# Attention, out-projection and FFN of one encoder layer: the last gate norm in block 0's FFN, two output tiles' SSD halves ahead, and two gate products by token halves

## The chip, the cores and the metric

One core of one Trainium2 chip runs the whole program. The metric is the device time of one execution in microseconds; the time of a kernel is the median of its runs. A core has a matrix engine (PE), a vector engine (DVE), an activation engine (ACT), a general engine (POOL) and a queue engine (SP), which in this kernel only issues the DMAs. Each engine executes its own program in order and waits on semaphores of the others.

## The reference

One encoder layer over 2048 new frames and 32 running streams of one frame-step each. What matters here (`p` are the weights, names shortened):

```python
def mixer(h, k_past, v_past, ssm_h0, conv_prev, p):
    proj = h @ p['w_in']                  # q, k, v, z, x/B/C, dt
    ...
    attn = stick_breaking(q, q_pos, k_all, v_all, k_pos).reshape(b, l, D_ATT)
    ...
    y, h_fin = ssd_scan(xh, dt, a, bm, cm, ssm_h0)
    y = y + p['d_skip'][:, None] * xh
    y = rmsnorm(y * jax.nn.silu(z), p['g_ssm_out'])
    out = jnp.concatenate([rmsnorm(attn, p['g_attn_out']), y], axis=-1) @ p['w_out']
    ...
def conv_ffn(h, conv_prev, p):
    gu = h @ p['w_up']
    gate_c, conv_new = causal_dwconv(gu[..., :D_FF], conv_prev, p['ffn_conv_w'], p['ffn_conv_b'])
    return (jax.nn.gelu(gate_c, approximate=True) * gu[..., D_FF:]) @ p['w_down'], conv_new
...
x = x + rmsnorm(mixer(rmsnorm(x)))        # pre and post norm, each with its gain
x = x + rmsnorm(conv_ffn(rmsnorm(x)))
```

`D_MODEL` is 1024, `D_FF` 2816; 8 attention heads and 8 SSD heads of 64. The out-projection multiplies a row of 1024 values: 512 of attention and 512 of SSD.

## The kernel before

Tokens are cut into four blocks of 512, 512, 512 and 544 (the last holds the 32 running streams). Features lie on partitions, 128 at a time, tokens in the free dimension. Every large product is done in three matmuls of fp32r parts, high by high, high by low and low by high (`dense`, L173 to L186, the matmul is L180), so a product over 1024 inputs (8 pieces `k` of 128) is 24 matmuls for one tile of 128 outputs. Weights are split into parts once (`divide`: cast on ACT L160, subtraction on POOL L161, store L164) and read back from DRAM later (`recall`, L152).

`phase_in` (0 to 595 us) makes the input projections and the SSD of all blocks. What is left of it is the gate of block 3: `gate` multiplies by the weights of z, 32 steps of 6 matmuls of 128x272, and applies the gate; `gate_norm` (L680 to L706) squares, sums over partitions (L222), takes the power on POOL (L245), transposes back (L257), scales on DVE (L698), makes high and low parts on ACT and POOL (L702, L704) and stores both to `yS[3]` (L705, L706).

`heads(s)` is the attention of block s: slots of one head, one block of keys and 128 queries. A slot is scores (L914), a log-sigmoid pair on ACT (L759, L760), a scan (L762) and a product (L767) on DVE or POOL, transposes on PE (L933) that ACT casts and DVE subtracts from (L937, L938), and the products with v (L955), added to `att` on DVE (L970). Block 0 has 32 slots, block 1 64. Between slots `heads` takes steps of a filler, a generator that writes other work into the program; the number of steps per slot is a fixed rate: L1576 to L1594 give `heads(0)` the gate and the norm, 44 steps, and `heads(1)` the stream of block 0, 648. PE's products of a filler are pinned behind the attention's matmuls that precede them; each engine's order then comes from a scheduler that simulates the program.

`Tail.stream(0)`, the filler of `heads(1)`: `out_units` makes the 8 output tiles c of the out-projection for token half a, then for half b, each over k = 4..7 (SSD) and then 0..3 (attention, which needs all heads of block 0 and their norm). Half a's chain runs beside half b's products: `residual` (sums L222, transposes L257, scaling L1072 on DVE, addition L1077, store L1078), `split` (high part xhi on ACT L1107, low part xlo on DVE L1108) and `root` (second sums and power). Half b's chain then runs beside GAP = 24 empty steps (L1485 to L1489), and only then do the FFN's products begin, by `up(j)`: 22 pairs of gate product (PSUM tile `o`, two banks) and up product (tile `u`), then `down`. The gate product's result goes to `gb` on DVE (L1335) with r, the root of the norm, as a factor, so that it waits for both halves' `root`.

Lines that the diff touches stand in the profile under the numbers printed here.

## Time and profile before

| | us |
|---|---|
| median of three runs | 2865.14 |
| lowest, highest | 2861.31, 2866.26 |
| the profiled execution | 2866.48 |
| its span in the trace | 2864.7 |
| block 0's attention (from the first slot) | 595.02 to 686.99 |
| start of block 1's attention to the dense out-projection | 686.99 to 717.75 |
| sums of half a | 743.35 |
| end of half b's out products | 767.9 |
| first gate result (L1335), first up product | 805.23, 805.5 |

Over the span PE is busy for 97%, DVE 58%, ACT 43%, POOL 40%. A row of the timeline is one instruction or several equal ones in a row; the brackets at its end say how long the engine had been idle and what ended that. In tables by stage, "busy" counts an instruction from start to end at whatever clock PE had, and PEclk is the mean share of the full clock.

### The profile page before, as it was taken

To read this page: it belongs to the slowest core of one execution; us is meant where nothing else is said; L and a number is where in the kernel's file an instruction comes from. 1 tells how busy PE (TensorE), PEld (TensorE's weight loads), DVE (VectorE), ACT (ScalarE), POOL (GpSimd) and SP (SyncE) were. 2 spreads that over 40 slices of the span, in tenths; PEclk is the share of its full clock that TensorE was granted. 3 is DMA by queue.
4 is the path that set the end of the run, shared out by engine and by line. 5 is a ranking of instruction groups with operands and counts; after the bars stand their busy time and mean duration, and the time that the engine had idled before them with its cause. 6 is when DMAs were issued, how large, how long until landed. Compare 5 with 4: busy or idle time off the path is not lost.

```text
span 2864.7 us, 45898 instructions
## 1 busy us (share of the span) xinstructions
PE 2772.8 (97%) x16673; PEld 2393.9 (84%) x16673; DVE 1648.3 (58%) x2628; ACT 1218.0 (43%) x2570; POOL 1142.8 (40%) x1075
## 2 busy tenths in 40 slices
PE   7999999998899999999999999999999999999998
PEld 6777879986878888897888888878888878899998
DVE  7684747368564455657555555876666653623334
ACT  5343434357655454555433334644444433321211
POOL 4633241325666565655322224553323224511113
PEclk9999999999999999999999999999999999999999
DMA  8879595997868877876655557665555555755554
GB/s 297 283 257 312 201 314 179 289 283 242 299 197 290 272 255 259 282 257 200 202 181 181 180 177 246 201 207 186 175 174 168 167 188 189 252 177 177 173 181 129
DMA packets 342083, 635.73 MB, mean 222 GB/s; under 512 B 73082, under 2 KB 188418, under 8 KB 332386
## 3 DMA queue, kind: packets, MB, share of 16 engines
q1 hardware_dynamic: 341282, 632.24, 67.8%
q8 instruction: 133, 2.18, 0.3%
q14 instruction: 92, 0.75, 0.1%
q10 hardware_dynamic: 576, 0.56, 0.1%
HBM read 476.11 MB, written 156.57 MB: 221 GB/s over the span
## 4 chain that ended last, share of the span: by engine, by line
PE 81%; DMA 7%; DVE 6%; issue 2%; ACT 2%; POOL 1%; SPq 1%; DVEq 0%; POOLq 0%; ACTq 0%
PE o L180 41%; PE u L180 13%; PE t L180 11%; PE z L914 4%; PE pa L955 4%; PE pt L933 3%; PE o L451 3%; DMA w<-wS_outw 1%; DVE prow L762 1%; DMA w<-wS_wq 1%; DMA acB<-acD 1%; DMA eA<-acD 1%; DMA w<-wS_outw_part 1%; DVE xlo L1108 1%; PE u L222 1%
## 5 line engine op out<-in xcount | busy, mean ns | idle before, releaser
L180 PE MATMUL o<-xhi,w 128*128 128x512 f32 (+2 forms) x3968 | 1038.9, 344 | 20.4 <-ACT xhi L353 7.9
L180 PEld LDWEIGHTS o<-xhi,w 128*128 128x128 f32 x3968 | 694.6, 191 | 112.4 <-ACT xhi L353 7.9
L180 PE MATMUL o<-xlo,w 128*128 128x512 f32 (+2 forms) x1984 | 681.0, 344 | 3.4 <-DVE xlo L354 1.2
L767 POOL TENSOR_TENSOR beta<-beta,prow 128x512 f32<-128x512 f32 (+3 forms) x256 | 256.1, 1001 | 505.2 <-DVE prow L762 443.2
L180 PEld LDWEIGHTS o<-xlo,w 128*128 128x128 f32 x1984 | 377.4, 190 | 48.2 <-DVE xlo L339 3.0
L180 PE MATMUL u<-xhi,w 128*128 128x512 f32 x1056 | 351.4, 398 | 0.0
L180 PE MATMUL o<-ah,w 128*128 128x512 f32 x992 | 341.7, 402 | 7.0 <-DVE f L1410 7.0
L1356 POOL TENSOR_TENSOR y<-y,gb 128x512 f32<-128x512 f32 (+1 forms) x88 | 115.8, 1315 | 445.6 <-ACT gb L1355 442.8
L161 POOL TENSOR_TENSOR w<-wraw,w 128x512 fp32r<-128x512 f32 (+3 forms) x180 | 244.5, 1361 | 122.4 <-ACT w L160 92.2
L938 DVE TENSOR_TENSOR wt<-pt,wt 128x512 fp32r<-128x512 f32 (+2 forms) x320 | 192.2, 602 | 150.2 <-ACT wt L937 148.7
L762 DVE TENSOR_TENSOR_SCAN prow<-gam,prow,z 128x513 f32<-128x513 f32 x192 | 245.3, 1278 | 55.5 <-ACT beta L760 55.2
L937 ACT CAST wt<-pt 128x512 fp32r<-128x512 f32 (+2 forms) x320 | 168.0, 526 | 234.3 <-PE pt L933 232.1
L180 PEld LDWEIGHTS u<-xhi,w 128*128 128x128 f32 x1056 | 198.6, 188 | 46.1
L180 PEld LDWEIGHTS o<-ah,w 128*128 128x128 f32 x992 | 187.1, 189 | 49.2 <-DVE f L1410 7.9
L180 PE MATMUL u<-xlo,w 128*128 128x512 f32 x528 | 209.1, 396 | 0.0
L180 PE MATMUL o<-al,w 128*128 128x512 f32 x496 | 196.9, 397 | 0.0
L759 ACT ACTIVATE gam<-z 128x512 f32<-128x512 f32 (+2 forms) x320 | 173.3, 542 | 52.3 <-PE z L914 28.5
L180 PE MATMUL t<-xhi,w 128*128 128x272 f32 x960 | 189.5, 293 | 6.1 <-DMA w<-wS_outw_part 3.4
L933 PE MATMUL pt<-ident,beta 128*128 128x128 f32 x1088 | 182.8, 277 | 1.8 <-DVE wt L938 1.0
L1348 DVE SCALAR_TENSOR_TENSOR y<-gb,cv,y 128x512 f32<-128x512 f32 (+1 forms) x176 | 143.9, 818 | 66.0 <-ACT y L1346 63.0
L160 ACT CAST w<-wraw 128x512 fp32r<-128x512 f32 (+3 forms) x180 | 113.5, 631 | 160.8 <-PE o L180 94.3
L955 PE MATMUL pa<-wt,v 128*64 128x256 f32 (+3 forms) x1152 | 171.4, 279 | 9.9 <-DVE wt L938 4.3
(290 smaller groups left out, 4846.6 us busy)
## 6 DMA issues: line engine op xcount, KB each, us to landing
w<-wS_up SPq DMA_DIRECT2D x264, 512.0 KB, 3.6
w<-wS_dn SPq DMA_DIRECT2D x144, 384.0 KB, 3.5
wS_up<-w SPq DMA_DIRECT2D x88, 512.0 KB, 3.3
w<-wS_outw SPq DMA_DIRECT2D x78, 512.0 KB, 6.3
wraw<-wup SPq DMA_DIRECT2D x88, 256.0 KB, 4.4
k<-kS SPq DMA_DIRECT2D x80, 256.0 KB, 3.8
v<-vS SPq DMA_DIRECT2D x80, 256.0 KB, 3.8
w<-wS_bx SPq DMA_DIRECT2D x18, 1024.0 KB, 4.9
```

The lines of the kernel that those rows point to most:

```text
L161: nc.gpsimd.tensor_tensor(lo, raw[:, :m, :], hi.bitcast(F32), op=ALU.subtract)
L180: mm = nc.tensor.matmul(ps[:, : c1 - c0], l, r, start=first and i == 0 and k == 0, stop=last and i == 2 and k == len(w) - 1, **({"skip_gro ...
L759: nc.scalar.activation(g[:, c0:512], z, AF.Sigmoid, scale=-0.125)
L762: nc.vector.tensor_tensor_scan(back(pr), back(g), z[:, 0:1].to_broadcast([P, n + 1]), self.kn.ones[:, 0:1] if prev is None else prev, op0= ...
L767: eng.tensor_tensor(b[:, :n], b[:, :n], pr[:, c0 + 1 : 513], op=ALU.mult)
L914: mm = nc.tensor.matmul(z[:, :n], q[:, P * b : P * b + P], k[:, :n], start=e == 0, stop=e == 1 and kc < s)
L933: mm = nc.tensor.transpose(t[:, P * j : P * j + P], w[:, P * j : P * j + P], kn.ident[:])
L937: nc.scalar.copy(hi, t)
L938: kn.exit = nc.vector.tensor_tensor(lo, t, hi.bitcast(F32), op=ALU.subtract)
L955: nc.tensor.matmul(av[:m, 2 * P * p + c0 : 2 * P * p + 2 * P], v[:, j, :m], wt[:, rest, j, c0:], start=kc == s and p + j + rest == 0, stop ...
L1348: nc.vector.scalar_tensor_tensor(y[:, :W], gb[:, i : i + W], kn.col(wc + i), y[:, :W], op0=ALU.mult, op1=ALU.add)
L1356: nc.gpsimd.tensor_tensor(y[:, :W], y[:, :W], t, op=ALU.mult)
```

## The change

Three things move.

1. The norm of block 3's gate. `gate` still fills block 0's attention (36 steps instead of 44), but each of its four tiles is stored to DRAM (`yG`); `gate_norm_last` loads them back as `gx` in two tiles of 272 tokens, and its steps (28 for both) are taken as `done` steps in block 0's FFN.
2. In `stream(0)`, after ten empty steps, `out_ahead` opens both `o` banks with output tiles 0 and 1: their SSD halves (k = 4..7) on all 512 tokens, then their attention halves by token halves. `out_units` makes the other six.
3. `gates` takes the place of the empty steps but eight: the gate products of j = 0 and 1 on the first 256 tokens, while half b's chain runs. `up(0)` and `up(1)` complete them on the last 256.

```diff
+        if s == NSB - 1:
+            nc.sync.dma_start(kn.yG[:, c, :], xc[:, c, :nt])
...
+def gate_norm_last(kn, tmp, pool):
+
+    nc, s = kn.nc, NSB - 1
+    for c0, c1 in tiles_of(SBS[s][1]):
+        n = c1 - c0
+        tile = lambda nm, bufs=1: pool.tile([P, n], F32, name=nm, bufs=bufs)
+        xs, sq = [], tile("gsq")
+        for c in range(4):
+            xs.append(tile("gx", 4))
+            nc.sync.dma_start(xs[c][:], kn.yG[:, c, c0:c1])
+            yield
+        for c, x in enumerate(xs):
+            yield
+            if c == 0:
+                nc.scalar.activation(sq[:], x[:], AF.Square)
+            else:
+                t = tile("gt")
+                nc.scalar.activation(t[:], x[:], AF.Square)
+                nc.gpsimd.tensor_tensor(sq[:], sq[:], t[:], op=ALU.add)
+        r = tile("gr")
+        for _ in kn.rstd_steps(tmp, *kn.bank, [sq], n, 512, out=r):
+            yield
+        for c, x in enumerate(xs):
+            yield
+            kn.spaced(nc.vector.scalar_tensor_tensor(
+                x[:], x[:], kn.col(C_GSSM + c), r[:], op0=ALU.mult, op1=ALU.mult
+            ))
+            hi, lo = (tile(nm, 2) for nm in ("ghi", "glo"))
+            hi, lo = hi[:].bitcast(F32R), lo[:].bitcast(F32R)
+            nc.scalar.copy(hi, x[:])
+            nc.gpsimd.tensor_tensor(lo, x[:], hi.bitcast(F32), op=ALU.subtract)
+            nc.sync.dma_start(kn.yS[s][0, :, c, c0:c1], hi.bitcast(F32))
+            nc.sync.dma_start(kn.yS[s][1, :, c, c0:c1], lo.bitcast(F32))
...
-        for i, c in enumerate(range(KC) if c0 == 0 and self.keep is None else back + list(range(back[0]))):
+        order = list(range(KC)) if c0 == 0 else back + list(range(back[0]))
+        if s == 0:
+            if c0 == 0:
+                yield from self.out_ahead(cat)
+            order = [c for c in order if c > 1]
+        for i, c in enumerate(order):
...
+    def out_ahead(self, cat):
...
+        n = SBS[0][1] // 2
+        open_ = []
+        for c in range(2):
+            w = kn.weight(kn.wp, kn.a["wout"][c], key=("outw", c, "part"))
+            ps = self.po[0].tile([P, 512], F32, name=self.po[1])
+            open_.append((w, ps))
+            for k in range(4, KC):
+                kn.dense(ps, w[k : k + 1], cat, 0, 2 * n, k0=k, first=k == 4, last=False, pin=self.pin, loose=True)
+                yield
+                yield
+        for c0 in (0, n):
+            for c, (w, ps) in enumerate(open_):
+                ps = ps[:, c0 : c0 + n]
+                for k in range(4):
+                    kn.dense(ps, w[k : k + 1], cat, c0, c0 + n, k0=k, first=False, last=k == 3, pin=self.pin, loose=True)
...
+    def gates(self):
...
+        self.pre = {}
+        for j in range(2):
+            w = kn.weight(kn.wp, kn.a["wup"][j], key=("up", j))
+            ps = self.po[0].tile([P, 512], F32, name=self.po[1])
+            self.pre[j] = w, ps
+            for k in range(KC):
+                kn.dense(
+                    ps, w[k : k + 1], self.x, 0, SBS[0][1] // 2, k0=k, first=k == 0, last=False, pin=self.pin, loose=True
+                )
+                yield
...
-        yield from islice(owed, 8)
+        yield from islice(owed, 8) if s else range(10)
...
-                for n, _ in enumerate(owed if s else range(GAP)):
+                for n, _ in enumerate(owed if s else chained(self.gates(), range(GAP - 2 * KC))):
...
-        done = iter(())
+        done = self.gate
...
-            out = att.heads(0, KC * 4 + 12, lambda i: i % 3 == 2 and next(sample, None))
+            out = att.heads(0, KC * 4 + 4, lambda i: i % 3 == 2 and next(sample, None))
```

Line numbers above L676 shift by some 30 (attention's L914 is L946 in the changed kernel, L933 is L965, L955 is L987, L900 to L928 are L932 to L960).

PE's program in the first slots of block 1's attention, before (`z` are scores, `pa` the products with v, `pt` transposes, `o` a product of the filler with the parts xhi and xlo of the out-projection's input):

```order
L180 MATMUL o<-xlo_7301,w 128x256
L180 MATMUL o<-xhi_7293,w 128x256
L914 MATMUL z<-k,qa 128x256
L914 MATMUL z<-k,qb 128x256
L918 LDWEIGHTS identb
L918 MATMUL z<-maskq,identb 128x128
L955 MATMUL pa<-wt,v 128x256
L955 MATMUL pa<-wt,v 128x128
L955 MATMUL pa<-wt,v 64x256
L955 MATMUL pa<-wt,v 64x128
L914 MATMUL z<-k,qa 128x384
```

and in the changed kernel:

```order
L950 MATMUL z<-maskq,identb 128x128
L180 MATMUL o<-xhi_7239,w 128x512
L180 MATMUL o<-xlo_7247,w 128x512
L180 MATMUL o<-xhi_7239,w 128x512
L180 MATMUL o<-xhi_7240,w 128x512
L180 MATMUL o<-xlo_7248,w 128x512
L180 MATMUL o<-xhi_7240,w 128x512
L180 MATMUL o<-xhi_7241,w 128x512
L180 MATMUL o<-xlo_7249,w 128x512
L180 MATMUL o<-xhi_7241,w 128x512
L180 MATMUL o<-xhi_7242,w 128x512
L180 MATMUL o<-xlo_7250,w 128x512
```

Before, twelve products of 128x256 end here and attention is alone from then on; in the change 24 products of 128x512 for two output tiles stand among the first three slots.

PE's program from the last out products of half b on, before:

```order
L180 MATMUL o<-xlo_7297,w 128x256
L180 MATMUL o<-xhi_7289,w 128x256
L955 MATMUL pa<-wt,v 64x256 x3
L955 MATMUL pa<-wt,v 64x128
L914 MATMUL z<-k,qb 128x512
L933 MATMUL pt<-ident,beta 128x128 x4
L914 MATMUL z<-k,qa 128x128
L914 MATMUL z<-k,qb 128x128
L918 LDWEIGHTS identb
L918 MATMUL z<-maskq,identb 128x128
L933 MATMUL pt<-ident,beta 128x128 x4
```

and in the changed kernel, where the products behind the scores are those of gate 0 (`gates`):

```order
L180 MATMUL o<-xlo_7246,w 128x256
L180 MATMUL o<-xhi_7238,w 128x256
L946 MATMUL z<-k,qb 128x512
L950 LDWEIGHTS identb
L950 MATMUL z<-maskq,identb 128x128
L946 MATMUL z<-k,qa 128x512
L946 MATMUL z<-k,qb 128x512
L180 MATMUL o<-xhi_7235,w 128x256
L180 MATMUL o<-xlo_7243,w 128x256
L180 MATMUL o<-xhi_7235,w 128x256
L180 MATMUL o<-xhi_7236,w 128x256
L180 MATMUL o<-xlo_7244,w 128x256
```

The first halves of the gate products come between the out products and the attention work that stood directly behind them.

SP's program at the end of block 0's attention, before, around the first stores of the norm (L705, L706; `qa`, `qb`, `k`, `v` are the loads of attention, `qS_83` belongs to block 1):

```order
L900 DMA qa<-qS_83 128x512
L902 DMA qb<-qS_83 64x512 x2
L909 DMA k<-kS_79 128x512
L928 DMA v<-vS_86 128x512
L705 DMA yS_96<-khi 128x544
L900 DMA qa<-qS_83 128x512
L909 DMA k<-kS_78 128x512
L902 DMA qb<-qS_83 64x512
L706 DMA yS_96<-klo 128x544
L902 DMA qb<-qS_83 64x512
```

and in the changed kernel, around the third store of the gate (L676) and the third load of the norm (L715), one head earlier:

```order
L934 DMA qb<-qS_82 64x512
L676 DMA yG<-xc 128x544
L934 DMA qb<-qS_82 64x512
L941 DMA k<-kS_78 128x512
L840 DMA sk<-ck 128x2x512
L960 DMA v<-vS_86 128x512
L715 DMA gx<-yG 128x272
L840 DMA sk<-ck 128x2x512
L833 DMA sv<-cvv 128x512 x3
L932 DMA qa<-qS_82 128x512
```

The stores of the norm no longer stand among the loads of block 1's first head; a store and a load of the gate stand among those of block 0's later heads.

## Rows read from the trace of the kernel before

**Rows 1.** The page's second part: PE's busy tenths in 40 slices of the span.
```profile
PE   7999999998899999999999999999999999999998
```

**Rows 2.** Busy time by stage: length; busy us (count), clock, DMA share, GB/s.
```profile
595.02:686.99 91.97, 84.02 (x684) 71.44 (x685) 67.43 (x107) 61.83 (x161) 38.92 (x51) 0.95 0.94 297
686.99:717.75 30.76, 25.59 (x166) 20.25 (x167) 26.98 (x54) 20.40 (x49) 18.37 (x21) 0.89 0.55 170
717.75:743.35 25.60, 24.90 (x210) 24.72 (x209) 3.98 (x9) 11.61 (x28) 15.11 (x17) 1.00 0.71 248
743.35:767.90 24.55, 23.43 (x192) 22.56 (x191) 20.15 (x28) 16.10 (x40) 17.89 (x18) 1.00 0.95 312
767.90:805.51 37.61, 30.27 (x170) 22.82 (x168) 31.32 (x49) 25.57 (x65) 24.48 (x29) 0.86 0.74 257
800.00:1200.00 400.00, 398.95 (x1905) 325.26 (x1905) 201.42 (x265) 204.36 (x423) 254.32 (x224) 1.00 0.77 260
```

**Rows 3.** The same, slots of block 0, last row block 1.
```profile
652.37:661.02 8.65, 7.84 (x73) 6.71 (x71) 7.31 (x13) 8.34 (x23) 7.13 (x10) 1.00 0.94 297
661.02:673.03 12.01, 10.08 (x84) 7.95 (x85) 9.07 (x15) 8.31 (x22) 6.86 (x7) 1.00 1.03 335
673.03:686.99 13.96, 10.46 (x93) 7.59 (x94) 11.07 (x16) 11.01 (x26) 7.08 (x8) 1.00 0.73 238
697.52:717.75 20.23, 17.59 (x104) 14.09 (x105) 18.09 (x35) 14.23 (x33) 11.37 (x14) 0.83 0.44 131
```

**Rows 4.** PE's timeline: start, us, instruction, [idle before <-releaser].
```profile
673.03 0.30 PE L914 MATMUL z<-k,qa 128*128 128x128 f32 x1 [1.50 <-DMA k<-kS]
678.96 0.44 PE L914 MATMUL z<-k,qa 128*128 128x384 f32 x1 [1.31 <-DVE sprow L762]
686.99 0.33 PE L914 MATMUL z<-k,qa 128*128 128x128 f32 x1 [1.46 <-DMA qb<-qS]
```

**Rows 5.** Groups of lines L698 and L704, 655 to 815 us: ns min/median/max, starts.
```profile
L698 DVE SCALAR_TENSOR_TENSOR xc<-xc,cv,rstd x4: 769/1082/1654, 679.3 to 688.2; 128x544 f32<-128x544 f32 x4
L704 POOL TENSOR_TENSOR klo<-xc,khi x4: 1148/1348/1634, 682.0 to 692.7; 128x544 fp32r<-128x544 f32 x4
```

**Rows 6.** SP's timeline; then DMA from 595 to 700 us: KB, us to landing.
```profile
673.96 0.33 SPq L928 DMA_DIRECT2D v<-vS  x1
681.36 0.32 SPq L705 DMA_DIRECT2D yS<-khi  x1
683.90 0.45 SPq L902 DMA_DIRECT2D qb<-qS  x1
...
DMA packets 17301, 30.11 MB, mean 287 GB/s; under 512 B 2727, under 2 KB 2866, under 8 KB 17289
yS<-klo SPq DMA_DIRECT2D x4, 272.0 KB, 3.5
```

**Rows 7.** Chain that ended last: 24 products of 128x512 of the first up.
```profile
805.76 5.60 PE u L180 x24
```

**Rows 8.** PE's and DVE's timelines between half b's sums and the first up.
```profile
771.79 1.28 DVE L762 TENSOR_TENSOR_SCAN prow<-gam,prow,z 128x513 f32<-128x513 f32 x1 [4.27 <-ACT beta L760]
772.29 0.74 PE L955 MATMUL pa<-wt,v 128*128 128x256 f32 x4 [1.85 <-ACT wt L937]
776.95 1.02 DVE L762 TENSOR_TENSOR_SCAN prow<-gam,ones,z 128x385 f32<-128x385 f32 x1 [1.52 <-ACT beta L760]
802.46 0.69 DVE L938 TENSOR_TENSOR wt<-pt,wt 128x512 fp32r<-128x512 f32 x1 [0.73 <-ACT wt L937]
```

**Rows 9.** Low parts (L1108), both halves; and six of half a on DVE's timeline.
```profile
L1108 DVE SCALAR_TENSOR_TENSOR xlo<-n,cv,xhi x16: 454/1310/1553, 752.2 to 795.6; 128x256 fp32r<-128x256 f32 x16
755.27 7.58 DVE L1108 SCALAR_TENSOR_TENSOR xlo<-n,cv,xhi 128x256 fp32r<-128x256 f32 x6
```

**Rows 10.** A sum and its power in block 1's FFN: PE and POOL.
```profile
1363.92 0.50 PE L222 MATMUL u<-ones,fsq 128*128 128x1 f32 x4
1365.34 0.72 POOL L245 TENSOR_TENSOR rn_v<-rn_v,mhalf 128x2 f32<-128x2 f32 x1
1366.67 0.39 PE L257 MATMUL u<-ident,rn_v 128*128 128x128 f32 x2
```

More of the change, by code (lines that the diff above doesn't have):

```diff
@@ L639, in phase_in @@
         if last:
[L640 to L643 removed]
+            return lambda tm: gate(kn, s, xs, xc, None, tm)
         bufs = {"khi": 2, "klo": 2, "t": 2, "sq": 1, "zc": 2}
@@ L692, in gate_norm @@
     r = rstd(sq, nt, 512)
-    for _ in range(rests):
-        yield
     for c in range(4):
         yield
-        n = xc[:, c, :nt] if s == NSB - 1 else tm("zc")[:, :nt]
-        kn.spaced(nc.vector.scalar_tensor_tensor(
+        n = tm("zc")[:, :nt]
+        nc.vector.scalar_tensor_tensor(
             n, xc[:, c, :nt], kn.col(C_GSSM + c), r[:, :nt], op0=ALU.mult, op1=ALU.mult
-        ), s == NSB - 1)
+        )
         hi = tm("khi")[:, :nt].bitcast(F32R)
@@ L1039, in out_units @@
             nc.scalar.copy(m, ps[:, : c1 - c0])
-            if i < KC - 1 or c0 == 0:
-                att.square(self.msq[:, c0:c1], m, i == 0)
+            if i < len(order) - 1 or c0 == 0:
+                att.square(self.msq[:, c0:c1], m, i == 0 and s > 0)
                 self.msqs = [self.msq[:, c0:c1]]
@@ L1313, in up @@
         W = 546 if last else 512
-        raw = []
-        def halves(c):
-            if s:
-                return kn.weight(kn.wp, kn.a["wup"][c], key=("up", c))
-            raw.append([kn.raw(kn.a["wup"][c][:, i : i + UNIT, :], UNIT) for i in (0, UNIT)])
-            return [w for i in (0, 1) for w in kn.divide(kn.wp, raw[-1][i], UNIT, ("up", c, UNIT * i) if c < NJ or i or 1 not in FAST else None)]
-        wg = halves(j)
+        halves = lambda c: kn.weight(kn.wp, kn.a["wup"][c], key=("up", c))
+        pre = self.pre.pop(j, None) if s == 0 else None
+        wg = pre[0] if pre else halves(j)
         gb = self.yp.tile([P, 548], F32, name="gb")
@@ L1327, in up @@
         for c0, c1 in tiles_of(nt):
-            ps = self.po[0].tile([P, 512], F32, name=self.po[1])
+            ps = pre[1] if pre else self.po[0].tile([P, 512], F32, name=self.po[1])
+            h = nt // 2 if pre else 0
             for k in range(KC):
-                kn.dense(ps, wg[k : k + 1], self.x, c0, c1, k0=k, first=k == 0, last=k == KC - 1, pin=self.pin)
+                kn.dense(
+                    ps[:, h:], wg[k : k + 1], self.x, c0 + h, c1, k0=k, first=not h and k == 0, last=k == KC - 1,
+                    pin=self.pin, loose=bool(h),
+                )
                 if k < KC - 1:
@@ L1357, in up @@
         wu = halves(NJ + j)
-        if s == 0 and FAST:
-            for i, t in self.sums(j, *raw).items():
-                d = self.raws[j, i] = kn.dp.tile([P, 4, P], F32, name=f"sS_{j}_{i}")
-                nc.sync.dma_start(d[:], t[:])
         for c0, c1 in tiles_of(nt):
@@ L1560, in build @@
         kn.yS = [dp.tile([2, P, 4, n], F32, name=f"yS{s}") for s, (_, n) in enumerate(SBS)]
+        kn.yG = dp.tile([P, 4, SBS[NSB - 1][1]], F32, name="yG")
         kn.acD = [dp.tile([40, P], F32, name=f"acD{s}") for s in range(NSB)]
@@ L1575, in build @@
         late = ssd.enter_context(tc.tile_pool(name="ssd_tmp", bufs=2, reuse_waits="tile", side="right"))
-        att.filler = chained(*rest(lambda nm: late.tile([P, 544], F32, name=nm, bufs=1 if nm == "sq" else 2), late))
+        att.filler = rest(lambda nm: late.tile([P, 544], F32, name=nm))
         with ExitStack() as c2:
             sample = att.sample(c2, pu)
-            out = att.heads(0, KC * 4 + 12, lambda i: i % 3 == 2 and next(sample, None))
+            out = att.heads(0, KC * 4 + 4, lambda i: i % 3 == 2 and next(sample, None))
             for _ in sample:
@@ L1584, in build @@
         tail = Tail(kn, att, ctx, pu)
+        c2 = ExitStack()
+        tail.gate = gate_norm_last(kn, att.tmp, c2.enter_context(tc.tile_pool(name="late_g", bufs=1, reuse_waits="tile")))
         for s in range(NSB):
@@ L1589, in build @@
             else:
+                c2.close()
                 att.inner.close()
```

17 lines of the change are left out of this document (11 added, 6 removed).

## The prediction

> **What bounds the kernel now.** First the page's forty slices of 71.6 us: PE shows 9 nearly everywhere, but 8 in the tenth and eleventh, 645 to 788 us [rows 1]. A gain of any size has to come from such a place. Second, the busy time by stage [rows 2]. A steady piece of block 0's FFN reads 398.95 of 400 us on PE, with DVE at half: there PE is the bound, and a microsecond of PE work that is taken out of it is a microsecond less. For the other stages I count as lost the length less busy time times granted clock (clock 1.00 is 2.4 GHz; the share below it is the time at 1.2). That gives 30.76 - 25.59 x 0.89 = 8.0 us between the start of block 1's attention and the dense run of out-projection products, 0.7 and 1.1 in the two halves of that run, and 37.61 - 30.27 x 0.86 = 11.6 from its end to the first up product at 805.51. Third, the last twelve slots of block 0's attention [rows 3]: 0.8 + 1.9 + 3.5 = 6.2 us lost. Together 27.6 us in 153. Fourth, what ended PE's waits there [rows 4]: a load of k, a scan on DVE, a load of qb. DVE reads 26.98 of 30.76 and 31.32 of 37.61 us where PE loses most [rows 2], so in these two stages DVE sets the pace and PE work can be put into them free, as long as the products are ready and DVE gets nothing new. In FFN the reverse holds. This is the exchange that the change makes.
>
> **Block 0's attention (652 to 687 us).** The filler steps of this stage fall from 44 to 36 over 34, so the gate products (32 steps of 6 matmuls) end in slot 26 rather than 21. Five slots, about 30 matmuls, leave slots in which PE had no gap and go to slots where it loses 1.9 to 3.5 us per four. The norm leaves as well: four scalings on DVE (1.08 us at the median, up to 1.65) and four subtractions on POOL (1.35) [rows 5], and eight stores on SP. The first of these stores waited for the scaling, and SP issued nothing between 673.96 and 681.36; the loads of qa and qb for block 1 stood behind it, and the qb issued at 683.90 is the one that PE waited 1.46 us for at 686.99 [rows 4, 6]. What comes in: four stores of yG, which wait only for the gate products, and four loads of gx, which wait for these stores to land. A store of that size took 3.5 us at the median [rows 6], and the order has five rows of SP between a store and its load at the closest, so a load may hold the q and k loads behind it for a microsecond or two; a k load of this stretch was already 1.50 us late [rows 4]. DMA is also full here (share 1.03) [rows 3], and three stores and three loads of half the size are 3 x 272 + 3 x 136 KB = 1.25 MB, at the 287 GB/s of the whole stage 4.4 us of transfers [rows 6]. Bounds: all 6.2 us back, or nothing back and 4.4 lost. I take +4.0: the qb wait (1.5) goes for certain, and of the 4.7 us left somewhat over half, because the products fill gaps and the norm's DVE and POOL work is gone, which lies nearer to the upper row.
>
> **Start of block 1's attention (687 to 718).** Before, PE has 12 products of 128x256 in the first slot, ten more just ahead of the dense run, and between them attention alone, since a tile's attention half needs the finished heads. After, 24 products of 128x512 (5.60 us for 24 [rows 7]) stand in the first three slots, and the attention halves of the same two tiles (48 of 128x256, half as long each, again 5.6) among the later slots: 11.2 us of work where 2.6 stood, in a place that loses 8.0. It is taken from the dense run, which is PE at full pace. Order also has 21 attention slots there where 13 stood, so DVE gets more as well, but that is attention which otherwise would lie in FFN, where DVE is half idle. With more products among the slots the granted clock, 0.83 from 697.5 to 717.75 [rows 3], should stay nearer to 1.00. Bounds: all 8.0; or 3.6, if each added slot brings the loss of the slots here with it (8.0 over 13 is 0.62 a slot, 13.0 over 21, less the 8.6 us of added products, leaves 4.4). I take +6.5, nearer the top, since the 24 products need only what block 0's SSD left long ago and two PSUM banks that are free, and the lower row counts the slow clock in full.
>
> **From the sums of half a (743.35) to the first up product (805.51).** Here the change puts 48 products of 128x256, 5.6 us, directly behind the out products of half b, in place of attention slots, and 24 of 128x512 (gate 0) shrink to 24 of 128x256; PE's work in this stretch grows by some 0.7 us net. But DVE carries both chains. Order shows three more full scans (1.28 us each), three more weight subtractions (0.69) and one more addition to the attention sum (about 0.69) on it ahead of the first gate result: 6.6 us [rows 8]. DVE's idle pieces between the chains are 4.27, 1.52 and 0.73, 6.5 together [rows 8]; I let half of them take the new work, which leaves 3.3 us. Are the gate halves ready? They need the low parts of half a (L1108). Those came 8.8 to 19.4 us after the sums, six of them one after another in 7.58 us, 1.26 each [rows 9]. Half b's out products now end some 16.5 us after the sums instead of 24.5 (48 products fewer, 5.6 us, and about 2.4 us less of attention among them), so gate 0, 2.8 us long, wants the last low part at some 19: half a microsecond of PE wait, in time that DVE bounds anyway. So I take -3.0, bounds +2 (all of DVE's new work falls into its idle time and the chain of half b starts earlier) and -6.6.
>
> **The norm in FFN.** Six one-column products, six small transposes, two powers and about 14 more POOL instructions of 272 columns come between up products. PE work is unchanged in sum: it was counted in the stage it left. A sum with its power in block 1's FFN took 2.75 us from the ones product to the transposes, and PE had products between them all the way [rows 10]. POOL reads 254.32 of 400 us [rows 2] and has room. I take -0.5, bounds 0 and -3.0 (two norms at 1.5 us, what a wait would be if the power came behind one POOL subtraction of 1.35).
>
> **Sum.** +4.0 + 6.5 - 3.0 - 0.5 = 7.0 us less. The profiled execution took 2866.48 us, so 2859.5; the median of the runs is 1.3 us under it, and I predict 2865.14 - 7.0 = 2858.1.
>
> **Rivals.** *A: the gain is eaten in the gap, about 2863.* For it: DVE is busy in 31.32 of the last 37.61 us [rows 2], and the sixteen low parts took between 0.45 us, where POOL paused, and 1.55 beside its work [rows 9]. Order now puts six of the weight splits (L161, POOL) beside chain a. If all eight low parts take 1.55, that is 12.4 us; now the first two took 0.45 and 1.55 and the rest 7.58, 9.6 in all, so the last comes 2.8 us later, and PE, which executes in order, stands in front of gate 0 with attention's transposes queued behind it, so DVE starves in turn. -3.0 becomes -5.8, and with half of the first term gone (2.0) the sum is 2.2 us less, 2863. The Trainium skill, page "SBUF — State Buffer", section "Who interferes with whom", states that a DVE instruction with two SBUF inputs contends with a GpSimd instruction that reads SBUF, since the second input comes through an interface that the two share; the rows agree, 0.45 against 1.26 to 1.55 us, and by this rule the change chooses a bad neighbour for chain a, and the sum would be A's. Against it: six of the eight are slow already. *B: slower, about 2872.* The same place, one mechanism: PE's order. The transposes that DVE's attention work needs stand behind the gate halves (5.6 us), the halves behind the last low part (0.5 + 2.8 us), and DVE's next step behind a cast on ACT like the one that PE waited 1.85 us for at 772.29 [rows 8]. If nothing covers that, DVE idles for 5.6 + 3.3 + 1.85 and has its 6.6 us of new work still to do: 17.3 us in place of 3.0, so 7.0 - 14.3 = 7.3 slower, 2872. It decides from 78 us on between the two marks (62.2 now). Against it: the scans of two slots are ready before the gate halves start. *C: all goes well, about 2850.* 6.2 + 8.0 + 2.0 = 16.2, 2849. *D: the change doesn't bite*, because attention ends later by what PE saves; that is a weak one, since FFN is bound by PE and every product done earlier is one fewer there.
>
> **How the numbers follow.** My forecast (2854 to 2862) 0.50, A 0.23, B 0.14, C 0.10, D 0.03. The bounds add to 2849 and, the other way, to 4.4 + 6.6 + 3.0 - 4.0 = 10 slower, 2875. Leaving out most of B and a little of C, the range is 2850 to 2868. A measurement of this kernel tells about 0.2% (5.7 us) from nothing. Faster means under 2859.4: seven tenths of my own case and C, 0.45. Same: the rest of my case, A and D, 0.41. Slower: B, 0.14.
>
> **What would show it.** In the profile after: no qb wait at the start of block 1's attention, and busy shares of PE over 8.5 of 10 in the eight slots before it; 24 products of 128x512 in its first slots and less than 2 us lost there; from the sums of half a to the first up product 64 to 67 us; FFN of block 0 still at 10 of 10. What would prove me wrong: k, q or v loads waiting behind gx on SP; PE waiting more than 3 us for xlo or for DVE's scans behind the gate halves; a granted clock under 0.8 in the gap; PE waiting for the power in FFN.

## The result: 15 us slower, and the profile after

The changed kernel takes 2880.19 us (median of 7 runs, 2871.28 to 2885.05), the kernel before 2865.14 (2861.31 to 2869.32): ratio 1.0050, 95% interval 1.0038 to 1.0062. The forecast was 2858.1 with a range of 2850 to 2868; the time lies above it, and above rival B's 2872. The profiled execution took 2885.05 us, the longest of the seven.

The page's PE slices, to hold against [rows 1]: the two 8 of the tenth and eleventh slice are gone, and the twelfth (793 to 865 us) now has one. By this view alone the change looks like a gain.

```profile
PE   8999999999989999999999999999999999999998
```

Busy time by stage of the changed kernel (columns as in [rows 2]); the stretches are block 0's attention, four pieces from block 1's first slot to the sums of half a, half b's products, the rest up to the first up product, and the FFN around the norm:

```profile
595.00:683.77 88.77, 82.38 (x669) 69.86 (x670) 64.48 (x101) 57.60 (x154) 33.01 (x44) 0.94 0.97 317
683.77:695.70 11.93, 11.85 (x77) 9.21 (x75) 6.17 (x16) 5.99 (x16) 3.88 (x6) 1.00 0.37 120
695.70:712.68 16.98, 13.49 (x77) 10.44 (x77) 15.87 (x32) 11.35 (x27) 6.99 (x8) 0.80 0.51 153
712.68:731.13 18.45, 16.26 (x121) 14.46 (x121) 14.75 (x23) 14.74 (x37) 13.32 (x18) 1.00 0.32 101
731.13:752.81 21.68, 21.54 (x182) 21.37 (x181) 2.17 (x3) 8.59 (x20) 10.10 (x12) 1.00 0.70 245
752.81:767.85 15.04, 14.60 (x123) 14.31 (x122) 11.01 (x16) 9.58 (x26) 12.22 (x13) 1.00 0.78 253
767.85:819.68 51.83, 41.17 (x263) 35.89 (x261) 46.87 (x69) 35.06 (x86) 33.35 (x35) 0.87 0.68 228
845.00:855.00 10.00, 7.27 (x31) 5.91 (x30) 7.95 (x13) 4.80 (x12) 6.93 (x7) 0.83 0.91 298
```

By the prediction's measure (length less busy time times clock) the four pieces from 683.77 to 752.81 lose 0.1, 6.2, 2.2 and 0.1 us, 8.6 in all. The same measure on the kernel before, cut at the same events (the fourth piece, the dense run, is the third row of [rows 2]):

```profile
686.99:695.84 8.85, 7.30 (x57) 5.62 (x58) 7.31 (x14) 5.55 (x15) 6.95 (x7) 1.00 0.89 287
695.84:712.25 16.41, 12.90 (x69) 9.80 (x70) 14.65 (x33) 10.20 (x25) 6.51 (x8) 0.79 0.50 148
712.25:717.75 5.50, 5.38 (x41) 4.83 (x41) 5.01 (x9) 4.65 (x11) 4.91 (x7) 1.00 0.15 49
```

With the dense run they lose 1.6, 6.2, 0.1 and 0.7: also 8.6. The stretch in the middle, attention alone on PE with DVE at nine tenths, is the same before and after. PE's timeline says why (start, us, instruction, idle before and what ended it):

```profile
684.73 0.48 PE L180 MATMUL o<-xhi,w 128*128 128x512 f32 x1
...
691.80 0.40 PE L180 MATMUL o<-xhi,w 128*128 128x512 f32 x1
...
712.68 0.38 PE L180 MATMUL o<-xhi,w 128*128 128x256 f32 x1 [0.43 <-ACT xhi L894]
...
722.73 0.38 PE L180 MATMUL o<-xhi,w 128*128 128x256 f32 x1 [1.61 <-ACT xhi L894]
```

The 24 SSD products ran from 684.73 to 692 us, ahead of the slots that starve. The next product is an attention half at 712.68, and it waits for the parts of the last heads' norm.

In the gap, loss went from the 12.7 us of [rows 2] to 0.4 + 16.0 = 16.4. PE now stands in front of half a's and half b's low parts; the last two of these rows are half b:

```profile
769.83 0.38 PE L180 MATMUL o<-xlo,w 128*128 128x256 f32 x1 [0.50 <-DVE xlo L1170]
771.25 0.39 PE L180 MATMUL o<-xlo,w 128*128 128x256 f32 x1 [0.46 <-DVE xlo L1170]
774.09 0.58 PE L180 MATMUL o<-xlo,w 128*128 128x256 f32 x1 [1.86 <-DVE xlo L1170]
...
795.58 0.38 PE L180 MATMUL o<-xhi,w 128*128 128x256 f32 x1 [1.10 <-ACT xhi L1169]
...
805.50 0.58 PE L180 MATMUL o<-xlo,w 128*128 128x256 f32 x1 [3.30 <-DVE xlo L1170]
```

In block 0's FFN the norm's power stands on POOL behind two weight splits, and the transposes, with all of PE's products behind them, wait for it. That is the 7.27 of 10 at clock 0.83 above. POOL's timeline, and the wait of the transposes (L257):

```profile
843.58 2.97 POOL L161 TENSOR_TENSOR w<-wraw,w 128x512 fp32r<-128x512 f32 x2
846.51 1.30 POOL L245 TENSOR_TENSOR rn_v<-rn_v,mhalf 128x3 f32<-128x3 f32 x1
```

```profile
  POOL rn_v L245: 2.7, 1
```

**A ledger across kernels.** To compare places where work has moved, I count PE's program up to an event by shape, at durations of full clock (0.2333 us for 128x512, from the 24 in 5.60 of [rows 7]; attention's matmuls likewise), and take that from the time at which the event comes. Its zero is uncertain by a microsecond or two for a stretch (some come out under zero), so only differences in a row are read. Loss in us by stretch, from the profiled executions:

| stretch | before | changed | N: e1 | G+K: f4 | N+G+K: e7 | all: e9 | all, one tile: h1 | all, late: i1 |
|---|---|---|---|---|---|---|---|---|
| first attention slot to sums of half a | 31.8 | 30.7 | 27.2 | 30.3 | 28.8 | 29.8 | 33.2 | 25.9 |
| to the first up product | 16.3 | 20.3 | 16.5 | 13.4 | 16.5 | 19.8 | 16.4 | 19.6 |
| to the sums of block 1's attention | -1.6 | 4.2 | -0.1 | -0.9 | 1.0 | 4.1 | 1.4 | 0.7 |
| to block 1's sums of half a | 1.3 | 5.9 | 1.9 | 3.1 | 1.3 | 5.7 | 4.7 | 2.6 |
| to the sums of block 3's attention | 26.4 | 33.5 | 26.4 | 27.3 | 24.4 | 27.5 | 25.6 | 26.6 |
| to the end | 23.6 | 20.9 | 25.4 | 17.5 | 16.7 | 18.8 | 18.8 | 21.3 |

The changed kernel against before: -1.1, +4.0, +5.8, +4.6, +7.1, -2.7. The +7.1 is chance for the most part: e9 is the same program and shows +1.1.

### The profile page after: what moved, and what is told of

It is laid out like the page before. It is cut to its first block, busy times and chain, and to the rows that moved or that the text cites. A ratio compares the mean times of both kernels' runs of the same rounds, so it can differ in the third digit from the quotient of the medians.

```text
span 2883.3 us, 45995 instructions
## 1 busy us (share of the span) xinstructions
PE 2784.5 (97%) x16700; PEld 2403.0 (83%) x16700; DVE 1654.1 (57%) x2635; ACT 1218.2 (42%) x2578; POOL 1147.6 (40%) x1083
## 4 chain that ended last, share of the span: by engine, by line
PE 64%; DVE 5%; DMA 2%; issue 1%; ACT 1%; POOL 1%; SPq 0%; DVEq 0%; POOLq 0%; ACTq 0%
PE o L180 30%; PE u L180 12%; PE t L180 11%; PE pa L987 3%; PE z L946 3%; PE pt L965 3%; DVE prow L794 1%; DMA w<-wS_outw 1%; DVE xlo L1170 1%; DVE f L1515 1%; PE u L222 1%; DVE n L1134 0%; DVE wt L970 0%; DVE f L1480 0%; DVE f L1522 0%
## 5 line engine op out<-in xcount | busy, mean ns | idle before, releaser
L965 PE MATMUL pt<-ident,beta 128*128 128x128 f32 x1088 | 182.2, 277 | 0.9 <-DVE wt L970 0.8
L987 PE MATMUL pa<-wt,v 128*64 128x256 f32 (+3 forms) x1152 | 173.2, 282 | 5.3 <-DVE wt L970 3.1
```

The costliest lines, as they stand in the source:

```text
L965: mm = nc.tensor.transpose(t[:, P * j : P * j + P], w[:, P * j : P * j + P], kn.ident[:])
L987: nc.tensor.matmul(av[:m, 2 * P * p + c0 : 2 * P * p + 2 * P], v[:, j, :m], wt[:, rest, j, c0:], start=kc == s and p + j + rest == 0, stop ...
```

## The experiments

N is the norm in FFN, O the tiles ahead with their ten empty steps, G the gate halves. The diff has a fourth part, K, which the prediction had not seen: its new `order` expression also drops a condition on `self.keep`, so that block 3's half a takes its tiles in the order 0 to 7 instead of 5, 6, 7, 0 to 4. Each diff is against the changed kernel, where nothing else is said. All ratios are to the kernel before on the same chip, with 95% intervals.

### Each part alone: e1_norm, e2_ahead, e3_gates, e6_order3

Each takes its hunks of the change and leaves the others out. For K alone against the kernel before:

```diff
-        for i, c in enumerate(range(KC) if c0 == 0 and self.keep is None else back + list(range(back[0]))):
+        order = list(range(KC)) if c0 == 0 else back + list(range(back[0]))
+        for i, c in enumerate(order):
```

N: 

> Only the norm of block 3's gate moves: out of block 0's attention, to DRAM and back, into block 0's FFN; no tiles ahead, no gate halves. Theory 1 (the power on POOL stands behind weight splits): one of the two norms shows PE waiting 2 to 3 us for rn_v in front of the transposes and a granted clock near 0.8 just after; the attention stage is 1 to 4 us shorter, and the sum is 0 to 4 us slower, 2865 to 2869. Theory 2 (the loss is in the gap and in the later blocks, not here): no wait at the power that costs anything, 2 to 4 us faster, about 2862.

O: 

> Only the two output tiles' SSD halves ahead, after ten empty steps, and the order of the other tiles in block 0; norm and gate products as before. Theory 1: PE's added products fill the first slots, but the attention halves now stand right behind the last head's norm and wait for its parts xhi (1 to 2 us), so start of block 1 and dense run together gain 0 to 2 us: 2863 to 2866. Theory 2 (as the prediction had it): 5 to 7 us faster, 2858 to 2860. Theory 3: the ten empty steps shift block 1's attention against the stream, and the block 1 boundary loses 4 to 5 us: 2868 to 2871.

G: 

> Only the gate products of j = 0 and 1 by token halves in the gap, with the weight order that goes with them. Theory 1: PE waits 2 to 3 us for low parts of half a and as much for those of half b, DVE stays full, the stretch from the sums of half a to the first up product is 64 to 67 us for 62.2 with about 7 us more PE work in it: 0 to 4 us faster, 2861 to 2865. Theory 2 (PE's order starves DVE): that stretch is over 72 us and the kernel 3 to 8 us slower, 2868 to 2873.

K: 

> Only the order of the out-projection's eight tiles in block 3's first token half, which the change's new expression for the order alters too (0 to 7 instead of 5, 6, 7, 0 to 4 once weights are kept). The prediction had not counted it. Theory 1: the profile of the change is 3 to 4 us better between the last head and the first sums of block 3, so 2 to 4 us faster, 2861 to 2863. Theory 2: the first tiles then need weights that were not loaded ahead, 1 to 3 us slower.

Measured: N 0.9989 [0.9980, 0.9998], O 1.0015 [1.0005, 1.0025], G 0.9979 [0.9971, 0.9988], K 0.9982 [0.9969, 0.9994]. Three of the four are gains, and O alone costs 4 us. N comes out as its second theory had it and O at the time of its third; G and K are a little faster than either of their theories gave. N saves 4.6 us up to the sums of half a (31.8 to 27.2 in the ledger); its transposes in FFN wait 0.4 us here. G alone takes the gap's loss from 16.3 to 12.8.

K is a wait and what follows it. The largest of PE's waits between the sums of block 3's attention and those of its half a, before (us in all, times, longest):

```profile
PE t L180 <- DMA w<-wS_outw_part: 3.4, 2, 2.7
```

and the busy time of that stretch, first before, then with G and K (f4), which has no wait there:

```profile
2363.60:2400.20 36.60, 33.09 (x225) 31.89 (x225) 1.95 (x7) 9.36 (x23) 11.29 (x15) 0.86 0.51 183
```

```profile
2360.60:2388.70 28.10, 28.10 (x225) 27.86 (x225) 1.95 (x7) 8.75 (x22) 9.19 (x12) 1.00 0.58 211
```

The same 225 rows of PE take 8.5 us less. Only 3.5 of it is idle time (36.60 less 33.09); the other 5 are products at a lower clock (0.86). With K alone the stretch is 30.2 us long and also free of waits. In the changed kernel the stretch is 30.2 us as well, but one load of `wS_outw` holds PE 2.9 us just ahead of it.

### One part missing: e4_no_norm, e7_no_ahead, e8_no_gates, and all again: e9_all

```diff
e7  -            if c0 == 0:
e7  -                yield from self.out_ahead(cat)
e7  -            order = [c for c in order if c > 1]
e8  -                for n, _ in enumerate(owed if s else chained(self.gates(), range(GAP - 2 * KC))):
e8  +                for n, _ in enumerate(owed if s else range(GAP)):
```

e4 has the norm back in block 0's attention with its old 44 steps; e7 also leaves the ten empty steps out.

Without N: 

> The whole change without its norm part: the norm is back in block 0's attention. The three other parts alone gave +0.15% (tiles ahead), -0.21% (gate halves) and -0.18% (block 3's order), together -0.24%. Theory 1 (the norm in FFN costs only beside the gate halves, whose weight splits crowd POOL just then): 0.998, about 7 us under the kernel before. Theory 2 (tiles ahead and gate halves don't go together: the halves follow half b's products sooner, before the low parts of half a are ready): 1.003 to 1.005, as slow as the whole change.

Without O: 

> The whole change without the two tiles ahead and the ten empty steps: norm in FFN, gate halves, block 3's order. Parts alone sum to -0.11 - 0.21 - 0.18 = -0.50%. Theory 1 (norm beside gate halves): 1.000 to 1.002, with a wait of 2 to 3 us for the power. Theory 2 (tiles ahead beside gate halves): 0.995 to 0.997, and no wait for the power over 1 us.

Without G: 

> The whole change without the gate halves: the gap holds 24 empty steps and FFN starts with full gate products; norm in FFN, tiles ahead, block 3's order. Parts alone sum to -0.11 + 0.15 - 0.18 = -0.14%. Both theories name the gate halves as one partner, so both expect 0.997 to 1.000; 1.003 or more would say that norm and tiles ahead are the pair.

All: 

> The whole change again, beside the others on one chip: 1.004 to 1.006 by every theory; the question is only how much of it each of the three kernels that leave one part out still shows.

Measured: without N 1.0036 [1.0023, 1.0048], without O 0.9978 [0.9965, 0.9990], without G 1.0026 [1.0014, 1.0038], all 1.0048 [1.0031, 1.0064]. O is the part that turns the change: it costs 0.0070 on top of N, G and K (e9 less e7, 20 us), and 0.0068 on top of G and K (e4 less f4, below), against 0.0015 alone. N, a gain alone, adds 0.0012 where O is in (e9 less e4), within the intervals.

e4 and e7 come out near the theory that tiles ahead and gate halves don't go together, e7 with a wait of 1.5 us for the power. e8 doesn't fit it: without G the kernel should have taken 0.997 to 1.000 by both theories, and it lies above that. O's price doesn't need the gate halves. Without them the gap reads

```profile
752.50:819.25 66.75, 53.76 (x336) 46.20 (x334) 58.17 (x84) 45.10 (x111) 45.46 (x47) 0.85 0.73 244
```

which loses 21.1 us by the prediction's measure, more than the changed kernel's 16.4. Beside N, G can cost in FFN instead: PE waits 1.5 us (e7) and 2.7 us (e9) for the norm's power, and 0.4 us or nothing without G (e1, e8).

What O brings into the gap shows on DVE. Its costliest groups from the sums of half a to the first up product, in the changed kernel (before: 17.2, 8.9, 8.5 and 5.7 us of low parts, scans of 513, subtractions and other scans):

```profile
L1170 DVE SCALAR_TENSOR_TENSOR xlo<-n,cv,xhi 128x256 fp32r<-128x256 f32 x16 | 17.9, 1162 | 0.0
L794 DVE TENSOR_TENSOR_SCAN prow<-gam,prow,z 128x513 f32<-128x513 f32 x8 | 10.1, 1268 | 0.6 <-ACT beta L792 0.5
L970 DVE TENSOR_TENSOR wt<-pt,wt 128x512 fp32r<-128x512 f32 (+3 forms) x17 | 9.8, 583 | 4.3 <-ACT wt L969 4.3
L794 DVE TENSOR_TENSOR_SCAN prow<-gam,ones,z 128x513 f32<-128x513 f32 (+3 forms) x9 | 8.2, 915 | 0.0
```

and with N, G and K but no tiles ahead (e7):

```profile
L1166 DVE SCALAR_TENSOR_TENSOR xlo<-n,cv,xhi 128x256 fp32r<-128x256 f32 x16 | 15.3, 995 | 0.0
L794 DVE TENSOR_TENSOR_SCAN prow<-gam,prow,z 128x513 f32<-128x513 f32 x7 | 8.8, 1269 | 0.0
L970 DVE TENSOR_TENSOR wt<-pt,wt 128x512 fp32r<-128x512 f32 (+3 forms) x13 | 7.6, 604 | 0.2 <-ACT wt L969 0.2
L794 DVE TENSOR_TENSOR_SCAN prow<-gam,ones,z 128x129 f32<-128x129 f32 (+3 forms) x6 | 4.7, 784 | 0.0
```

46.0 against 36.4 us, 9.6 more: four scans and four subtractions of attention that stood elsewhere, and slower low parts. e8 has the same 17 scans and 17 subtractions in its gap without G. So O brings this work with or without G, and why O costs so little alone (0.0015) is open. Over the whole stretch DVE is busy for 58 of 66.3 us with all parts (e9) and 49.2 of 63.2 without O (e7).

### The norm's power given room: e5_spaced, f3_no_ahead_spaced

```diff
         for _ in kn.rstd_steps(tmp, *kn.bank, [sq], n, 512, out=r):
-            yield
+            for _ in range(6):
+                yield
```

> The whole change, with six filler steps instead of one between the power on POOL and the transposes on PE in the norm that runs in FFN. In the whole change's profile PE waited 2.7 us there behind two weight splits on POOL, and the granted clock fell for some 4 us after it; from the first up product to block 1's last attention sums it lost 5.7 us more than the kernel before. Theory 1 (that wait is the norm's price): the wait is gone, this stretch loses under 2 us, and the kernel is 3 to 6 us under the whole change, 1.003. Theory 2 (the price is POOL's and DVE's extra work as such): nothing gained, 1.005.

> Norm in FFN with the spaced power, gate halves, block 3's order; no tiles ahead. The kernel without the spacing had 0.9978 (0.9965 to 0.9990), with 2.6 us more lost between the first up product and block 1's last attention sums. Theory 1: 0.996 to 0.997, the best of all. Theory 2: as without the spacing, 0.998.

Measured: the whole change so spaced 1.0010 [1.0001, 1.0019], without O 0.9988 [0.9977, 0.9999]. In e5 the power stands at 844.0 us and the transposes at 853.8, with no wait. From the first up product to block 1's attention sums the ledger loses 0.0 instead of e9's 4.1. The kernel gains more, 0.0038, and the rest of that lies in later blocks where nothing was edited. Without O the spacing gains nothing (e7 0.9978; f3 lies above both of its theories): what POOL has in front of the power depends on which weight splits fall there, and e1 waits 0.4 us, e7 1.5, the changed kernel 2.7.

### The ten empty steps: f1_no_empty

```diff
-        yield from islice(owed, 8) if s else range(10)
+        yield from islice(owed, 8)
...
-                ... - (22 - GAP if s == 0 else 0)
+                ... - (32 - GAP if s == 0 else 0)
```

> The whole change without the ten empty steps ahead of the two tiles (and ten steps fewer in the count that sets the rate). All kernels with tiles ahead lost 5.5 to 6.2 us between block 1's last attention sums and its first sums of half a, those without 1.3 to 3.3. Theory 1 (the empty steps shift block 1's stream against its attention): that stretch falls back to 1 to 3 us and the kernel gains 3 to 5 us, 1.003 to 1.004. Theory 2 (the tiles ahead themselves do it, by pulling work out of the places behind them): no change there, 1.004 to 1.006.

Measured 1.0036 [1.0024, 1.0048], not told apart from e9; its ledger reads 30.5, 20.9, 3.7, 6.9 in the first four rows. The empty steps are not the cost.

### Gate halves and block 3's order alone: f4_gates_order3, and with the gates later: h4_best_late

h4 and h3 have one line changed:

```diff
-                for n, _ in enumerate(owed if s else chained(self.gates(), range(GAP - 2 * KC))):
+                for n, _ in enumerate(owed if s else chained(range(GAP - 2 * KC), self.gates())):
```

> Gate halves and block 3's order alone; norm and tiles as in the kernel before. Theory 1 (the two are far apart in the program, so that their effects add): -0.21 - 0.18 = -0.39%, 0.995 to 0.997. Theory 2 (block 3's order gave its gain by chance of timing): 0.998, as the gate halves alone.

> Gate halves and block 3's order alone (0.9968 with the gates first), with the eight empty steps before the gate halves. Here half b's dense products cover most of half a's chain already. If the cover matters, the later gates gain little: 0.996 to 0.998. If the halves are better placed later in any case, 0.995 or less.

Measured: f4 0.9968 [0.9957, 0.9979], 2855.48 us, the fastest of all kernels here, faster than before and than the change; h4 0.9973 [0.9964, 0.9982]. The place of the eight empty steps doesn't matter.

### The gates later in the whole change: h3_late_gates

> The whole change, but the eight empty steps stand before the gate halves instead of behind them, so that attention goes first while half a's low parts are made. If PE's standing in front of the gate halves for a late low part (6.1 us in four waits in the profile of the changed kernel) is what the gap loses, that wait falls under 2 us and the stretch from the sums of half a to the first up product from 66.3 us to 62 to 64; kernel 1.0035 or less. If DVE's sum of work sets the stretch, it stays at 66 and the waits only change their names; kernel 1.005.

Measured 1.0035 [1.0024, 1.0047]; the gap is 67.5 us long and PE waits 6.4 us for low parts. This run can't tell the two theories apart: PE's and ACT's programs came out the same as in the changed kernel, since the scheduler places these products alike. It serves as a third run of the changed order: 1.0050, 1.0048, 1.0035.

### One tile ahead: h1_one_tile, h2_one_no_norm

```diff
-        for c in range(2):
+        for c in range(1):
...
-            order = [c for c in order if c > 1]
+            order = [c for c in order if c > 0]
```

> The whole change with one output tile ahead instead of two; the other seven are made in order. With two tiles the whole change took 1.0048 of before, with none 0.9978. If the price comes from the products that are taken out of the dense run (cover for half a's chain gone), it goes with their number: about 1.0015 to 1.002, and the loss from the sums of half a to the first up product lies between 16.5 us (none) and 19.8 (two). If it comes from having any attention half right behind the last head's norm, one tile costs nearly what two do, 1.004 or more.

> The same without the norm's move (one tile ahead, gate halves, block 3's order). Two tiles: 1.0036; none: 0.9968. Price by the number of tiles: 1.000. Price of any tile ahead: 1.003. If one tile gains what the prediction expected of two at the start of block 1's attention and costs nothing behind it: 0.995.

Measured: 1.0014 [1.0006, 1.0023], halfway between none (0.9978) and two (1.0048); and 0.9989 [0.9979, 1.0000], between 0.9968 and 1.0036. In sum the price goes with the number of tiles, but it doesn't lie where the cover theory put it. In h1's gap no product waits for a low part any more, and the loss there is that without tiles (16.4 against 16.5). By the ledger h1 loses 4.4 us more than e7 up to the sums of half a and 3.4 more at block 1's start. Only in h2, without N, does one tile cost in the gap (17.1, f4 13.4). So the cover theory is not shown.

### The SSD halves later: i1_late_halves, i2_one_late

```diff
-        yield from islice(owed, 8) if s else range(10)
+        yield from islice(owed, 8) if s else range(40)
...
                 kn.dense(ps, w[k : k + 1], cat, 0, 2 * n, k0=k, first=k == 4, last=False, pin=self.pin, loose=True)
-                yield
-                yield
+                for _ in range(4):
+                    yield
...
-                ... - (22 - GAP if s == 0 else 0)
+                ... - (-24 - GAP if s == 0 else 0)
```

i2 is h2 with 40 and six steps (and -24).

> The whole change with 40 empty steps instead of ten ahead of the two tiles and four steps instead of two for each piece of their SSD halves, so that these 24 products lie among the slots that in the changed kernel ran from 695.7 to 712.7 us with attention alone (PE busy 13.49 of 16.98 us at clock 0.80). If the prediction's term failed only because the products stood ahead of the starved slots, that stretch loses 3 to 4 us less: from block 1's first slot to the sums of half a the loss falls from 13 us to 9 or 10, and the kernel goes from 1.0048 to about 1.0035. If DVE's work there sets the pace and products among it only push attention back, the loss stays at 12 to 13 and the kernel at 1.0045 to 1.005.

> Gate halves and block 3's order with one tile ahead (0.9989), its SSD half behind 40 empty steps and with six steps for each piece, so that its 12 products lie in the starved slots. Placement as the cause: 0.998 or less, at best the 0.9968 that the same kernel takes with no tile ahead. Price by the number of tiles whatever the place: 0.999.

Measured: i1 0.9992 [0.9983, 1.0000]; i2 1.0012 [1.0002, 1.0022]. Busy time of i1 from block 1's first slot on: the first products of scores, the starved slots with the 24 products, the rest up to the dense run, the dense run, and the gap:

```profile
685.89:687.35 1.46, 1.07 (x9) 0.78 (x8) 1.46 (x4) 1.37 (x6) 0.86 (x1) 1.00 0.43 100
687.35:708.20 20.85, 18.80 (x119) 15.03 (x119) 16.40 (x38) 12.34 (x31) 8.25 (x11) 0.92 0.42 134
708.20:724.95 16.75, 16.22 (x120) 14.35 (x121) 15.99 (x26) 15.10 (x38) 12.58 (x16) 1.00 0.46 134
724.95:747.42 22.47, 21.65 (x183) 21.48 (x182) 1.69 (x3) 8.53 (x21) 11.98 (x15) 1.00 0.77 256
747.42:811.41 63.99, 52.60 (x371) 48.23 (x369) 55.18 (x81) 42.50 (x106) 43.16 (x45) 0.89 0.69 230
```

The 24 products now lie in four pieces from 689.6 to 704.6 us. Up to the first attention half (708.20) i1 loses 0.4 + 3.6 = 4.0 us, the changed kernel 0.1 + 6.2 = 6.3; up to the sums of half a 5.3 against 8.6. That is the gain expected of the place, though a part of it may come of less attention in this stretch: 17 products of scores for each of `qa` and `qb` instead of 19. The gap still loses what two tiles cost there (19.6 in the ledger, e9 19.8). The kernel gained more than expected: its norm waits only 0.3 us and block 1's start loses 2.6 instead of 5.7, neither of them edited, together 6.5 us. So i1 bears out the place by its stretch, and less by its total.

i2, above both of its theories, shows that the place is not enough. Up to the sums of half a it loses 1.3 less than h2, but then one load holds half b's products:

```profile
768.68 0.38 PE L180 MATMUL o<-xhi,w 128*128 128x256 f32 x1 [3.61 <-DMA w<-wS_outw]
```

and the gap's loss goes from 17.1 to 20.6. In a later stretch, up to block 3's attention, it loses 5.9 more than h2, which I can't explain.

## Why the prediction was wrong, point by point

In the ledger the four terms (+4.0, +6.5, -3.0, -0.5) came to +1.4, -0.3, -4.0 and -5.8, and a further 4.6 us went at block 1's start. The step that failed most is the second.

**Block 0's attention, +4.0: right in kind, 1.4 found.** The qb wait and the k wait of [rows 4] are gone. SP stood 2.8 us in front of one gx for its store to land, as feared, but PE waits for no load of block 1's first heads. The last three pieces before 683.77 read

```profile
651.50:660.00 8.50, 8.50 (x79) 7.41 (x77) 7.41 (x13) 7.12 (x20) 4.31 (x6) 1.00 0.85 264
660.00:672.00 12.00, 11.93 (x116) 10.44 (x114) 10.11 (x15) 9.46 (x25) 5.61 (x7) 1.00 1.01 342
672.00:683.77 11.77, 9.62 (x69) 6.82 (x68) 8.73 (x13) 7.58 (x18) 5.57 (x7) 0.86 1.05 344
```

3.6 us lost against the 6.2 of [rows 3], 2.6 less: the gate products did fill the gaps, but not in the last 12 us. Over the whole stage the ledger gives only 1.4 (19.0 to 17.6).

**Start of block 1's attention, +6.5: this step failed, 0 found.** The prediction counted 11.2 us of products "in a place that loses 8.0", and took the place as one. Of the loss, 6.2 lies in 16 us of attention alone; the 24 products fell ahead of these, where 1.6 was to be had and was had, and the 48 attention halves behind them, where they wait for ACT's parts (0.43, 1.61) and lose 2.2. The lower bound of 3.6 was wrong for the same reason. What spoke against the term stood in the prediction's own sentence that attention halves need the finished heads: with two PSUM banks held by tiles that can't go on, no other product is left to fill. i1 bears out the place: with later products this start loses 5.3 us instead of 8.6. It is not the whole of it, since one tile at that place (i2) takes off only 1.3.

**The gap, -3.0: right in size, its cause in part.** 62.2 became 66.9 us (64 to 67 expected), and the loss grew by 3.7. DVE's busy time in it grew by 6.4 us (51.5 to 57.9), with three scans more, close to the 6.6 counted. But the low parts of half a came later than the half microsecond of PE wait that was counted. In the changed kernel

```profile
L1170 DVE SCALAR_TENSOR_TENSOR xlo<-n,cv,xhi x16: 452/1488/1520, 761.6 to 808.8; 128x256 fp32r<-128x256 f32 x16
766.83 8.62 DVE L1170 SCALAR_TENSOR_TENSOR xlo<-n,cv,xhi 128x256 fp32r<-128x256 f32 x6
```

the last one of half a ends 22.6 us after the sums, 3.1 later than before (19.5 by [rows 9]; rival A had 2.8), and PE stood 0.50 + 0.46 + 1.86 = 2.8 us for them. All eight of half a ran beside POOL's work and took 1.5 us each; of half b's eight, four took 0.45 to 0.47 us, and beside three of these POOL had nothing to do. By the Trainium skill, page "SBUF — State Buffer", section "Who interferes with whom", a DVE instruction with two SBUF inputs contends with a GpSimd instruction that reads SBUF; the trace agrees, with 452 ns for the fastest low part and 1488 at the median of the changed kernel's sixteen.

The reverse side was left out: G alone is a gain of 3.5 here, and it is O that turns it. One term for two parts hid a gain of one and a loss of the other, 6.5 us apart in e4 against f4 (19.9 and 13.4). That O does this by taking 5.6 us of half b's cover away and leaving more attention for the gap is argued: the added scans speak for it, and h1, which takes half as much away and loses nothing there, against it.

**The norm, -0.5: the mechanism was named, the size was wrong.** The bound of -3.0 was two norms at 1.5 us, one POOL subtraction ahead of the power. In the run there were two splits of 1.49 us, for one of the two norms, 2.7 us, and products at a lower clock after it. The ledger has 5.8 more than before for that stretch, of which e5 takes away 4.1 (against e9). POOL's 254 of 400 us [rows 2] said that there is room in the mean, not at the one instant when PE stands in front of the power.

**What the prediction had not counted.** Block 1's start, 400 us later, loses 5.5 to 7.0 us in every kernel with two tiles ahead at the early place, and 1.3 to 3.1 without tiles. With O alone (e2) PE's waits there read

```profile
PE o L180 <- DMA w<-wS_outw_part: 1.8, 1, 1.8
PE z L914 <- DMA k<-kS: 1.4, 1, 1.4
PE o L180 <- DVE att L861: 1.4, 1, 1.4
```

where before has one of 0.2 us. Loads come late while DMA is full (share 1.06 in both kernels), but why O moves them is open: i1 with two tiles loses 2.6 there, and with one tile h1 loses 4.7 and h2 1.6. And K, hidden in one expression, gave 3 to 5 us back (0.9982 alone; 0.9979 to 0.9968 on top of G) that the forecast didn't have. **The rivals:** B's sign was right and its place wrong; the gap never came near 78 us. A's mechanism, slow low parts beside POOL with PE standing in front of gate 0, is real and was counted with too little weight. Of what would prove me wrong, the wait of over 3 us for xlo (3.30) and the wait for the power both came true.

**Two slips of the prediction** don't change its outcome. The slower end of its bounds takes 4.0 for the start where its own lower bound is 3.6, so that end is 10.4 us slower, not 10. And the time at 1.2 GHz is twice the share that the granted clock lacks of 1.00, since 1.2 is half of 2.4; the sums use the granted clock alone and stand.

**Open:** why O costs 0.0070 beside the other parts and 0.0015 alone; block 1's start; the half of i1's and e5's gains that lies in stretches not edited; and some 6 us of the changed kernel's own profile between block 1's sums of half a and block 3's attention, which e9, the same program, doesn't show.

## What to carry to other kernels

A stage that loses 8 us is not one hole: cut it at the events that the new work waits for, and fill only the piece in which that work is ready. Work moved ahead is gone from where it stood, so ask which chain ran beside it there; here two tiles ahead gained nothing in front of the starved slots, and the gap lost 3 to 7 us more with them than without (e9 against e7, e4 against f4). Read a diff's conditions for what they drop elsewhere, and time a change of several parts by its parts: three gains and one loss stood here as one slower kernel.

## What the runs showed of the hardware

- A wait costs more than its length where it lowers the clock: in block 3, 3.5 us of idle time came with products at a granted clock of 0.86 over 36.6 us, and the same 225 rows took 28.1 us at 1.00 without it.
- The clock follows what PE does in a stretch, not the stage: the slots ahead of the out-projection's first attention half had a granted clock of 0.79 (before) and 0.80 (changed) with attention alone, and 0.92 with 24 products of 128x512 among them (i1, cut a few slots earlier).
- One program, profiled three times (the changed kernel, e9, h3 on PE), took 2885.05, 2875.92 and 2870.22 us: two profiles that differ by up to 0.5% can be of one program.
